# Gate chunks by twos beside the retention: one base block in place of two

## The chip, the cores and the metric

The kernel runs on one core of a Trainium2 chip. The core has TensorE (matrix products, PE in the profile), VectorE (DVE), ScalarE (ACT), GpSimd (POOL) and SyncE (SP), which here issues most transfers. 16 DMA engines move data between the chip's main memory and SBUF. The metric is the time of one execution on the device in microseconds (us).

## The reference

One layer of a hybrid encoder over 256 tokens of width 2048, in float32. In short form below. A normalised input h goes through one wide projection into two token mixers, multi-scale retention (8 heads) and a gated delta rule (16 heads). Each mixer's output is gated by projections of h, and the two are merged by per-channel sigmoid gates. Cross-attention into 256 memory tokens and a squared-ReLU MLP follow.

```python
proj = h @ w_in
(rq, rk, rv, rg, gqkv, ga, gb, gz, gate_a, gate_b) = jnp.split(proj, np.cumsum(IN_SPLITS)[:-1].tolist(), axis=-1)
...
yr = silu(rg) * group_norm(retention(rope(rq), rope(rk), rv))
...
yg = silu(gz) * gated_rms_norm(gated_delta_rule(...))
merged = sigmoid(gate_a) * yr + sigmoid(gate_b) * yg
x = x + merged @ w_out
```

What matters here are the gate projections: h (256 x 2048) times the columns of `w_in` that make rg, gz, gate_a and gate_b, taken in chunks of 512 columns.

## The kernel before

Every float32 operand is split into two parts (`whi`, `wlo` for weights, a "quad" of high and low parts for tokens), and a product is three matmuls: high by high, high by low, low by high. A block of weights is 512 rows by 512 columns (1 MB). It comes by DMA as a tile `raw` of 128 partitions x 2048. ScalarE copies its halves to `whi`, VectorE subtracts for `wlo` (L990 and L991 in the code of this change), and TensorE multiplies 128 tokens by 512 columns at a time.

The mixer runs in four groups (`for j in range(5)`, the last turn only finishes). In each, the delta rule's blocks are projected, then the delta-rule gate of the group before, then `retention(j, yr)`, then `gate_retention(j, yr)`. The delta rule's own core (`gdn_core`) is a generator whose pieces run between the gate's products, a piece at each `step()`.

In groups 1, 2 and 3, and for the last delta-rule gate, the gate's two chunks of 512 columns are computed together by `two_chunks`. Let n be the chunk (0 or 1) and q the block of 512 rows of the weight (0 to 3); `load(n, q)` and `lines(n, q, h)` name such a block. Blocks q = 2 and 3 are multiplied in the plain way (`plain`). For q = 0 and 1 the two chunks and the two halves of the tokens form 2 x 2 blocks, and seven block products do the work of eight. Some take sums of tokens (`summed`, made beforehand by `sums_of_tokens`), some take sums of weight blocks. With b11 = (0, 0), b12 = (1, 0), b22 = (1, 1) and b21 = (0, 1) the weight sums are built in two tiles, each of two halves of 128 x 1024:

- x: first b12 + b11, then b22 is added (x2), then b21 (x4)
- y: b12 + b22

Three ways of building them occur. `load_parts` loads a block on SP's queue. `add_parts` has GpSimd issue a DMA that adds a block from main memory to what stands in the tile. `add_to` has VectorE add a block that is in SBUF anyway. The argument `moved` names the sums that go by adding DMA: in groups 1 to 3 these are x2, x4 and y, and x1 (b12 + b11) is VectorE's. In the last delta-rule gate x1, x2 and x4 go by DMA, and y is VectorE's.

The tiles have no room of their own: x and y take tags of tiles that are idle then. In groups 1 to 3, x has `kq` and `lw`, and y has `qk` and `tw` (`kq`: keys and queries of the delta rule; `lw`, `tw`: operands of its triangular solve; `qk`: queries and keys of the retention). In the last delta-rule gate x has `pairs` and `x_a`. A tile with `bufs=1` is given to its next user when its last reader is done; for `tw` the next user is the clearing on GpSimd (L765) for the following group's solve.

The order of each engine's instructions is worked out when the kernel is built, by a scheduler that simulates the engines. `tc.high_priority` moves loads, splits and additions forward, `tc.issue_after` keeps one instruction behind another. TensorE's order inside `two_chunks` is fixed by the list `ends`.

Lines to follow: L966 (load of a half on SP), L971 (adding DMA on GpSimd), L977 (VectorE's sum), L982 (load of `raw`), L990 and L991 (split), L998 (matmuls), L273 (a power on GpSimd, whose result VectorE needs at L858), L765 (clearing of `tw`).

Of the kernel before, what the change touches and what calls it, by code (L numbers as in the profile page):

```python
# [54 lines left out]
def trunk(ctx: ExitStack, tc: tile.TileContext, x_f, mem_f, positions, lead_f, small_f, w_blocks, w_chunks, w_ga,  # L55
# [3 lines left out]
    act, vec, pool, pe = nc.scalar, nc.vector, nc.gpsimd, nc.tensor  # L59
# [886 lines left out]
        vec.tensor_add(sv[:, 3], a12, sv[:, 1])  # L946
        split([a[:, i, :] for a in s_in], xs[:, 1, :])

    def two_chunks(chunks, evacs, before=None, moved=("x2", "x4", "y"), places=("kq", "lw")):

# [1 line left out]
        shared, p5 = bank("c"), bank("c")  # L954
        kept_back.append(None)
        x, y = ([mx.tile([P, 1024], F32, name=n + e, tag=tag, bufs=1) for e, tag in zip("ab", tags)]
                for n, tags in (("x", places), ("y", ("qk", "tw"))))
        opened, ends = set(), []

        def lines(n, q, h):  # L960
            return w_chunks[chunks[n], q][:, h * 1024:(h + 1) * 1024]

        def load_parts(to, n, q):
            with tc.high_priority(offset=100000), tc.issue_after(fetched[-1]):
                for h in range(2):
                    fetched.append(nc.sync.dma_start(to[h], lines(n, q, h)).ins)  # L966

        def add_parts(to, n, q):
            with tc.high_priority(offset=100000):
                for h in range(2):  # L970
                    pool.dma_start(to[h], lines(n, q, h), accum_op=ALU.add)  # L971

        def add_to(to, src):
            with tc.high_priority(offset=100000):
                for h in range(2):
                    with tc.issue_after(latest["lo"]):
                        vec.tensor_add(to[h], to[h], src[h])  # L977

        def load(n, q):
            raw = wp.tile([P, 4 * 512], F32, name="raw", tag="raw", bufs=3)  # L980
            with tc.high_priority(offset=100000):
                fetched.append(nc.sync.dma_start(raw, w_chunks[chunks[n], q]).ins)  # L982
            return raw[:, 0:1024], raw[:, 1024:2048]
# [25 lines left out]
        def plain(n, q, by_rows=False):  # L1009
            halves = parted(load(n, q))  # L1010
            for c, (i, t) in enumerate([(i, t) for t in range(NT) for i in range(4)] if by_rows else
                                       [(i, t) for i in range(4) for t in range(NT)]):
                ins = triple(own[n][t], [a[:, i, t * P:(t + 1) * P] for a in h1[q]],
                             [a[:, i % 2, :] for a in halves[i // 2]], (n, t))
                if c % 4 == 3:
                    ends.append(ins)
                    step()
# [18 lines left out]
                before(q)  # L1036

        plain(0, 2)
        load_parts(x, 1, 0)
        if "x1" in moved:  # L1040
            add_parts(x, 0, 0)
            load_parts(y, 1, 0)
        b11 = load(0, 0)
        product(shared, part(0, 0), b11, "shared")
        if "x1" not in moved:
            add_to(x, b11)
        with tc.high_priority(offset=50000):
            u = kept_sum("vh", shared)
        u1, u3 = u[:, 0], u[:, 1]
        product(p5, summed(0), x, "p5")  # L1050
        add_parts(x, 1, 1)
        plain(0, 3)
        if "x1" not in moved:
            load_parts(y, 1, 0)
        if "y" in moved:
            add_parts(y, 1, 1)
        b22 = load(1, 1)
# [1 line left out]
        product(shared, summed(1), x, "shared")  # L1059
        add_parts(x, 0, 1)  # L1060
        if "y" not in moved:
            add_to(y, b22)
        with tc.high_priority(offset=50000):
            d = kept_sum("vl", shared)
        others(1)
# [19 lines left out]
    def gates():  # L1085
# [22 lines left out]
        def of_retention(j, yr):  # L1108
            if j in (1, 2, 3):
                two_chunks((H_RG + j, H_TA + j), (silu_gate(yr), sig_gate(yr)))  # L1110
                return
            chunk(h1, cols(w_chunks, H_RG + j), silu_gate(yr))
            chunk(h1, cols(w_chunks, H_TA + j), sig_gate(yr))

        def of_delta_rule(j, yr, yg, quad, before=None):
            if j in (3,):
                spare.append(lambda: tuple(mx.tile([P, 1024], F32R, name=nm, tag=tag, bufs=1)
                                           for nm, tag in (("whx", "r4"), ("wlx", "g_a"))))
                two_chunks((H_GZ + j, H_TB + j), (silu_gate(yg), sig_gate(yg, yr)), before, ("x1", "x2", "x4"),
                           ("pairs", "x_a"))  # L1120
                spare.clear()
            else:
                chunk(h1, cols(w_chunks, H_GZ + j), silu_gate(yg))
                chunk(h1, cols(w_chunks, H_TB + j), sig_gate(yg, yr), before=before, cuts=2 if before else 1)
            to_feature(lambda t, f: yg[:, t, f * P:(f + 1) * P], quad)
# [190 lines left out]
    b11, b12, b22, b21 = (a[:, c:c + 8, :].rearrange("p k s -> p (k s)") for a in (rt, tr) for c in (0, 8))  # L1316
# [342 lines left out]
```

## Time and profile before

| what | value |
|---|---|
| median of 3 runs | 2033.4 us (2032.68 to 2033.46) |
| the profiled execution's own time | 2031.94 us |
| its span, first to last instruction | 2030.1 us |
| granted TensorE clock, mean | 0.999 |
| bytes moved by DMA | 422.03 MB, 208 GB/s on average |
| adding DMAs on GpSimd (L971) | 24 of 512 KB each |
| loads of halves on SP (L966) | 16 of 512 KB each, 4 each for xa, xb, ya, yb |
| VectorE's sums (L977) | 8, about 1.22 us each |

A row of the timeline gives the start in us from the beginning of the span, the length in us, engine, line, operation, output <- inputs (the ends a and b of x and y are their two halves), and in brackets the idle time before it with what ended it. "SPq" is the issue of a transfer on SP's queue. "DMA to landing" is the time from a transfer's issue to its arrival.

### The profile page before, as it was taken

Reading aid. Unit: us, or ns where it says so; the run is one execution under the profiler, and the core shown is the slowest. Engines: PE = TensorE matmul, PEld = TensorE weight load, DVE = VectorE, ACT = ScalarE, POOL = GpSimd, SP = SyncE. Lnnn points to the kernel's source line nnn. Section 1 sums busy time; section 2 is a strip of 40 time slices with the busy share of each in tenths; the row PEclk is TensorE's granted clock in tenths of the full one; section 3 lists DMA queues with packets and bytes.
Section 4 is the critical chain, followed back from the end, with each engine's and each line's share of the span. In section 5 each row is a group of like instructions: output and inputs, shape, how many; then the busy total and the mean of one; then the engine's idle time right before and its main releaser. Section 6 shows DMA issues by size and latency. Waiting matters only on the chain.

```text
span 2030.1 us, 28640 instructions
## 1 busy us (share of the span) xinstructions
PE 2019.0 (99%) x10742; PEld 1740.0 (86%) x10742; DVE 1617.3 (80%) x2507; ACT 1239.0 (61%) x2029; POOL 65.3 (3%) x73
## 2 busy tenths in 40 slices
PE   9999999999999999999999999999999999999998
PEld 7888888988888888888888899888888888888886
DVE  5887788879778887788887665777887887888788
ACT  6655765675567556755665565566557656656665
POOL 0000000000100010000200000000000000000000
PEclk9999999999999999999999999999999999999999
DMA  8578556455945585556976554567546546555661
GB/s 332 214 269 283 187 184 200 158 190 188 283 168 182 192 264 188 184 185 232 275 227 227 209 189 160 180 219 264 207 145 239 214 149 227 194 201 174 236 232 62
DMA packets 84683, 422.03 MB, mean 208 GB/s; under 512 B 17072, under 2 KB 25152, under 8 KB 40256
## 3 DMA queue, kind: packets, MB, share of 16 engines
q1 hardware_dynamic: 80656, 406.93, 57.3%
q0 software_dynamic: 3456, 12.58, 3.4%
q8 instruction: 84, 1.38, 0.3%
q10 hardware_dynamic: 432, 0.69, 0.1%
q14 instruction: 55, 0.45, 0.1%
HBM read 406.52 MB, written 11.55 MB: 206 GB/s over the span
## 4 chain that ended last, share of the span: by engine, by line
PE 96%; DVE 2%; DMA 1%; issue 1%; ACT 0%; SPq 0%; POOLq 0%; DVEq 0%; POOL 0%; ACTq 0%
PE s L217 51%; PE s L1404 8%; PE b L1404 7%; PE s L998 6%; PE s L174 5%; PE s L175 5%; PE s L173 5%; PE b L998 2%; PE s L406 1%; PE s L408 1%; PE s L407 1%; PE b L802 1%; PE b L145 1%; PE b L835 1%; PE b L144 1%; PE b L146 1%
## 5 line engine op out<-in xcount | busy, mean ns | idle before, releaser
L217 PE MATMUL s<-q,whi 128*128 128x512 f32 x2824 | 971.3, 391 | 0.0
L128 ACT ACTIVATE whi<-raw 128x1024 fp32r<-128x1024 f32 x535 | 567.3, 1061 | 419.6 <-PE s L217 219.1
L129 DVE TENSOR_TENSOR wlo<-raw,whi 128x1024 fp32r<-128x1024 f32 x535 | 652.0, 1221 | 214.2 <-ACT whi L128 210.5
L217 PE MATMUL s<-q,wlo 128*128 128x256 f32 x2824 | 765.0, 281 | 0.1
L217 PEld LDWEIGHTS s<-q,whi 128*128 128x128 f32 x2824 | 521.5, 188 | 100.6
L217 PEld LDWEIGHTS s<-q,wlo 128*128 128x128 f32 x2824 | 528.6, 188 | 13.6 <-DVE wlo L129 0.5
L174 PE MATMUL s<-wlo,q 128*128 128x512 f32 x448 | 176.3, 394 | 0.0
L175 PE MATMUL s<-whi,q 128*128 128x512 f32 x448 | 174.7, 390 | 0.0
L173 PE MATMUL s<-whi,q 128*128 128x512 f32 x448 | 158.9, 390 | 0.0
L226 ACT ACTIVATE bo<-s 128x256 f32<-128x256 f32 x192 | 73.1, 381 | 110.0 <-PE s L217 110.0
L1404 PE MATMUL s<-whi,q 128*128 128x512 f32 x384 | 122.1, 389 | 0.0
L227 DVE TENSOR_TENSOR bo<-bo,s 128x256 f32<-128x256 f32 x192 | 79.7, 415 | 41.0 <-ACT bo L226 40.6
L173 PEld LDWEIGHTS s<-whi,q 128*128 128x128 f32 x448 | 84.0, 188 | 17.5
L175 PEld LDWEIGHTS s<-whi,q 128*128 128x128 f32 x448 | 84.2, 188 | 16.7
L174 PEld LDWEIGHTS s<-wlo,q 128*128 128x128 f32 x448 | 84.2, 188 | 16.6
L1427 DVE TENSOR_TENSOR wlo<-rt,whi 128x1024 fp32r<-128x1024 f32 x55 | 67.4, 1225 | 35.8 <-ACT whi L1426 35.4
L998 PE MATMUL s<-whi,q 128*128 128x512 f32 x296 | 94.3, 390 | 0.0
L217 PE MATMUL s<-q,whx 128*128 128x512 f32 x248 | 86.6, 390 | 0.0
L1404 PEld LDWEIGHTS s<-whi,q 128*128 128x128 f32 x384 | 72.1, 188 | 15.0
L1426 ACT ACTIVATE whi<-rt 128x1024 fp32r<-128x1024 f32 x55 | 58.2, 1059 | 41.8 <-PE s L1404 29.4
L1404 PE MATMUL s<-wlo,q 128*128 128x512 f32 x192 | 74.7, 389 | 0.0
L991 DVE TENSOR_TENSOR wlo<-raw,whi 128x1024 fp32r<-128x1024 f32 x52 | 63.3, 1222 | 10.3 <-ACT whi L990 9.9
(427 smaller groups left out, 2970.7 us busy)
## 6 DMA issues: line engine op xcount, KB each, us to landing
raw<-w_ff SPq DMA_DIRECT2D x96, 1024.0 KB
raw<-w_chunks SPq DMA_DIRECT2D x76, 1024.0 KB
raw<-w_blocks SPq DMA_DIRECT2D x64, 1024.0 KB
raw<-w_xk SPq DMA_DIRECT2D x16, 1024.0 KB
raw<-w_out SPq DMA_DIRECT2D x16, 1024.0 KB
raw<-w_xq SPq DMA_DIRECT2D x16, 1024.0 KB
raw<-w_xo SPq DMA_DIRECT2D x16, 1024.0 KB
rt<-w_ff SPq DMA_DIRECT2D x16, 1024.0 KB
```

The lines of the kernel that those rows point to most:

```text
L128: latest["hi"] = act.activation(hi[:, cs], src[:, cs], AF.Copy).ins
L129: latest["lo"] = vec.tensor_sub(lo[:, cs], src[:, cs], hi[:, cs].bitcast(F32)).ins
L173: pe.matmul(o, xh, wh, start=first, stop=False)
L174: pe.matmul(o, xh, wl, start=False, stop=False)
L175: pe.matmul(o, xl, wh, start=False, stop=last)
L217: ins = pe.matmul(ps[b][:, :S] if part else ps[b], halves[h][part][:, i, b * P:(b + 1) * P], x[:, kk % 4, :], start=kk == 0 and not part, ...
L226: act.activation(o, ps[b][:, S:], AF.Copy)
L227: vec.tensor_add(o, o, ps[b][:, :S])
L991: latest["lo"] = vec.tensor_sub(lo, src, hi.bitcast(F32)).ins
L998: ins = pe.matmul(o, lhs[l], rhs[r], start=key not in opened, stop=False, skip_group_check=True).ins
L1404: ins = pe.matmul(o, lhs[l], rhs[r], start=key not in opened, stop=last and j == 2, skip_group_check=True).ins
L1427: latest["lo"] = vec.tensor_sub(lo, raw[:, c:c + 1024], hi.bitcast(F32)).ins
```

## The change

`two_chunks` gets the tags of both tiles as arguments. Where VectorE makes the first sum of x, the base block b12 is loaded once, into y, and VectorE writes x = y + b11 into x's tile, where before b12 was loaded into x, b11 was added in place, and b12 was loaded a second time, into y. GpSimd's addition of b22 to y then works on the tile that VectorE has read. In groups 1 to 3, y now has the tags `kq` and `lw`, and x has `qk` and `tw`. In the last delta-rule gate x1 still goes by DMA, so both loads stay; x keeps `pairs` and `x_a`, and y gets `kq` and `lw`. `add_to` becomes `add_of`, with any two sources.

```diff
-    def two_chunks(chunks, evacs, before=None, moved=("x2", "x4", "y"), places=("kq", "lw")):
+    def two_chunks(chunks, evacs, before=None, moved=("x2", "x4", "y"), places=("qk", "tw"), bases=("kq", "lw")):
...
-                for n, tags in (("x", places), ("y", ("qk", "tw"))))
+                for n, tags in (("x", places), ("y", bases)))
...
-        def add_to(to, src):
+        def add_of(to, *srcs):
             with tc.high_priority(offset=100000):
                 for h in range(2):
                     with tc.issue_after(latest["lo"]):
-                        vec.tensor_add(to[h], to[h], src[h])
+                        vec.tensor_add(to[h], *(src[h] for src in srcs))
...
         plain(0, 2)
-        load_parts(x, 1, 0)
         if "x1" in moved:
+            load_parts(x, 1, 0)
             add_parts(x, 0, 0)
-            load_parts(y, 1, 0)
+        load_parts(y, 1, 0)
         b11 = load(0, 0)
         product(shared, part(0, 0), b11, "shared")
         if "x1" not in moved:
-            add_to(x, b11)
+            add_of(x, y, b11)
...
         add_parts(x, 1, 1)
         plain(0, 3)
-        if "x1" not in moved:
-            load_parts(y, 1, 0)
         if "y" in moved:
             add_parts(y, 1, 1)
         b22 = load(1, 1)
...
         if "y" not in moved:
-            add_to(y, b22)
+            add_of(y, y, b22)
```

## The prediction

> **What bounds the kernel now.** I read the page first, then the chain of waits by engine, then busy time by windows over the places that the change touches. The page:
>
> ```profile
> span 2030.1 us, 28640 instructions
> ...
> PE 2019.0 (99%) x10742; PEld 1740.0 (86%) x10742; DVE 1617.3 (80%) x2507; ACT 1239.0 (61%) x2029; POOL 65.3 (3%) x73
> ...
> PE 96%; DVE 2%; DMA 1%; issue 1%; ACT 0%; SPq 0%; POOLq 0%; DVEq 0%; POOL 0%; ACTq 0%
> ```
>
> TensorE is busy for 99% of the span, and 96% of the chain that ended last is its own work. The edited code runs in four places: beside retention 1, 2 and 3 (calls 1, 2 and 3: from about 507, 721 and 937 us), and once in the last delta-rule gate. The view by windows, for call 2 and for calls 1 to 3 together, and then for stretches of call 1 with different transfers (columns: time, busy time of TensorE, its weight loads, VectorE, ScalarE, GpSimd, then granted clock, DMA share, GB/s):
>
> ```profile
> 721.00:791.00 70.00, 70.00 (x360) 59.55 (x359) 55.49 (x93) 43.95 (x74) 10.56 (x12) 1.00 0.77 235
> ```
>
> ```profile
> sum 197.00, PE 197.00 PEld 167.68 DVE 159.89 ACT 124.46 POOL 35.02; mean PE 65.67 PEld 55.89 DVE 53.30 ACT 41.49 POOL 11.67
> ```
>
> ```profile
> 530.00:534.50 4.50, 4.50 (x25) 3.83 (x24) 4.42 (x13) 2.02 (x3) 0.72 (x1) 1.00 1.05 187
> 536.00:538.50 2.50, 2.50 (x14) 2.04 (x14) 2.47 (x5) 1.80 (x3) 1.53 (x3) 1.00 1.08 380
> ```
>
> The three windows (507 to 576, 721 to 791, 953 to 1011) are 197.00 us long and TensorE is busy for 197.00 of them. The DMA engines are well filled too (a share of 0.77 in call 2), but nothing on TensorE waits for them. The last two rows price a transfer. From 530 to 534.5 only an adding transfer of GpSimd runs, at 187 GB/s; from 536 to 538.5 a plain load, at 380 GB/s. So one block (1.049 MB) costs 1.049/0.380 = 2.8 us of all engines when loaded and 1.049/0.187 = 5.6 us when added.
>
> A busy TensorE could hide slow matmuls, so I look at their spacing. Two pieces of the chain of waits, in order of time (start, length, instructions), the first where the DMA engines are full, the second where they are half idle, and the window of the second:
>
> ```profile
> 539.12 5.68 PE s L998 x25
> ```
>
> ```profile
> 569.92 6.60 PE s L998 x29
> ```
>
> ```profile
> 570.00:576.00 6.00, 6.00 (x28) 4.98 (x27) 5.33 (x10) 3.71 (x11) 1.01 (x1) 1.00 0.52 173
> ```
>
> 5.68/25 = 0.227 us and 6.60/29 = 0.228 us: traffic doesn't stretch them, so less traffic will not shorten them. (The Trainium skill, TensorE: Matmul & The Clock Gate, "Wait — 56ns, not 53.3ns?", gives 0.2157 us for a warm matmul of 512 columns; by that there would be 0.011 us in each matmul, whose cause the rows above show not to be the transfers.)
>
> **The change, part by part.** *Removed:* in calls 1 to 3 the second load of the base block (two halves, 512 KB each, into y). That is 2.8 us of the DMA engines in each call, 3.1 of 422 MB in all. TensorE waits for no transfer there, so this gives 0 us. What the load's absence moves: the plain loads behind it on SP's queue (the block of b22 first) can land earlier, and TensorE has no use for that.
>
> *Moved in place:* the two sums that VectorE writes. They were in place (x = x + b11), now x = y + b11 into other tiles.
>
> ```profile
> L977 DVE TENSOR_TENSOR xb<-xb,raw x3: 1217/1219/1221, 530.3 to 959.4; 128x1024 f32<-128x1024 f32 x3
> ```
>
> ```profile
> 762.50 1.23 DVE L991 TENSOR_TENSOR wlo<-xb,whi 128x1024 fp32r<-128x1024 f32 x1 [0.61 <-ACT whi L990]
> ```
>
> 1.219 us in place; the same engine's subtraction of this size into a third tile takes 1.23 us. Six instructions by 0.01 us, off TensorE's path: 0 us. The new tiles are those named qk and tw. In call 2 their last readers are long done when the second sum starts at 744.86 us (rows of the timeline, of SP, TensorE and VectorE):
>
> ```profile
> 716.80 0.34 SPq L775 DMA_DIRECT2D scr_t<-tw  x1
> ```
>
> ```profile
> 730.61 0.38 PE L903 MATMUL b<-qk 128*128 128x128 f32 x2
> ```
>
> ```profile
> 744.86 1.22 DVE L977 TENSOR_TENSOR xb<-xb,raw 128x1024 f32<-128x1024 f32 x1
> ```
>
> So VectorE gains no wait. In the last gate only y changes its tile, from the one that y of call 3 had to the one that it now has: the same release, 0 us.
>
> *Added wait 1.* GpSimd may add b22 into y only after VectorE has read y for x. Before, y was a tile of its own, and its addition ran ahead of the sum. GpSimd's rows in call 2, the start of the same addition in all calls, and the landing of x's addition:
>
> ```profile
> 742.13 0.85 POOL L971 DMA_DIRECT2D yb<-w_chunks  x1 [0.38 <-issue]
> ...
> 751.78 0.86 POOL L971 DMA_DIRECT2D xb<-w_chunks  x1 [0.96 <-DVE ve L924]
> ```
>
> ```profile
> L971 POOL DMA_DIRECT2D yb<-w_chunks x3: 852/857/877, 526.3 to 957.6; - x3
> ```
>
> ```profile
> L971 POOL DMA_DIRECT2D xb<-w_chunks x1: 860/860/860, 751.8 to 751.8; - x1
> ...
> DMA to landing us min/median/max: 8.8/8.8/8.8
> ```
>
> The second half of y's addition moves from 742.13 to 744.86 + 1.22 = 746.08 us, 3.95 us later; in call 1 from 526.3 to 531.5 (5.2), in call 3 from 957.6 to 960.6 (3.0). Behind it on GpSimd stands x's addition of b22 at 751.78; 4.9 us are left for an instruction of 0.86, so its issue doesn't move. But its transfer is behind y's on the DMA engines. It lands at 751.78 + 8.8 = 760.6 now. Who takes it, in call 2 (ScalarE's part of the split; VectorE's part is the row of 762.50 above; then the first matmul that needs it):
>
> ```profile
> 761.40 1.06 ACT L990 ACTIVATE whi<-xb 128x1024 fp32r<-128x1024 f32 x1 [0.86 <-PE s L998]
> ```
>
> ```profile
> 765.13 0.40 PE L998 MATMUL b<-wlo,sh 128*128 128x512 f32 x1
> ```
>
> ScalarE starts at 761.40, released by TensorE and not by the transfer: 0.8 us of slack. The split ends at 763.73, the matmul needs it at 765.13: another 1.4. TensorE therefore stalls only if x lands more than 2.2 us later than now. For calls 1 and 3:
>
> ```profile
> L971 POOL DMA_DIRECT2D xb<-w_chunks x1: 855/855/855, 537.3 to 537.3; - x1
> ...
> DMA to landing us min/median/max: 7.8/7.8/7.8
> ```
>
> ```profile
> 546.90 1.06 ACT L990 ACTIVATE whi<-xb 128x1024 fp32r<-128x1024 f32 x1 [0.86 <-PE s L998]
> ```
>
> ```profile
> L971 POOL DMA_DIRECT2D xb<-w_chunks x1: 867/867/867, 966.4 to 966.4; - x1
> ...
> DMA to landing us min/median/max: 8.6/8.6/8.6
> ```
>
> ```profile
> 975.91 1.06 ACT L990 ACTIVATE whi<-xb 128x1024 fp32r<-128x1024 f32 x1 [0.86 <-PE s L998]
> ```
>
> Landings 545.1 and 975.0, slack 1.8 and 0.9; with the same 1.4 behind it (the stages repeat to 0.01 us) TensorE stalls from 3.2 and 2.3 us.
>
> How much later will x land? No row shows it. *Lower end:* below nothing, -2.8 us in each call, if the removed load's engine time comes off the queue ahead of x; that is no gain for TensorE. *Upper end:* y's whole shift passes on, 5.2, 4.0 and 3.0 us, so stalls of 2.0, 1.8 and 0.7, together 4.5 us. Between them, if the shift passes on and the removed 2.8 us comes off it, x is 2.4, 1.2 and 0.2 us late. I take some 2 us in each call, nearest to the largest of these: the row of y's shift is the nearer one, since its addition now starts by its issue and not by the queue. 2 us is under all three limits: stall 0.
>
> *Added wait 2.* x now holds the tile tw until its last split. GpSimd clears tw for the next group as soon as y (its holder before) is split. Rows of GpSimd and VectorE in call 2:
>
> ```profile
> 777.21 0.94 POOL L765 MEMSET tw<- 32x1024 f32 x1 [12.33 <-DVE wlo L991]
> 778.28 1.03 POOL L273 TENSOR_TENSOR ro<-qe,nhalf_pow 128x4 f32<-128x4 f32 x1
> ```
>
> ```profile
> 780.51 1.12 DVE L858 SCALAR_TENSOR_TENSOR yg<-b,ro,small 128x128 f32<-128x128 f32 x4
> 781.55 1.22 DVE L991 TENSOR_TENSOR wlo<-xb,whi 128x1024 fp32r<-128x1024 f32 x1
> ```
>
> The clearing moves from 777.21 to 781.55 + 1.22 = 782.77 us. Queued behind it is ro, which yg waits for on VectorE, and yg stands ahead of that very split. In this order the two queues would wait for each other, so the scheduler has to put ro ahead of the clearing, which costs nothing, or yg behind the split (rival B). tw is next used by the following group's solve, tens of us later.
>
> *Sum:* 0 (load) + 0 (sums) + 0 (wait 1) + 0 (wait 2) = 0 us. The profiled execution took 2031.94 us (its span 2030.1 and 1.84 around it), 1.46 less than the median of the three runs, 2033.4 (2032.68 to 2033.46). The sum holds for either; I forecast the median, 2033.4 us.
>
> **The rivals.** *A, slower: x arrives late.* One mechanism, at the product of the third token sum with x, deciding from a landing 2.2 us later (call 2; 3.2 and 2.3 in the others). With the full shift passed on it costs 4.5 us. If x also has to share the engines with the next plain load, it costs one load's time more in each call:
>
> ```profile
> 738.46 17.47 SPq L982 DMA_DIRECT2D raw<-w_chunks  x3
> ```
>
> The third of these loads is issued at about 738.46 + 17.47 - 0.33 = 755.6, while x's addition is under way. Then x is 5.2, 4.0 and 3.0 plus 2.8 us late; less the limits 3.2, 2.2 and 2.3 this is 4.8 + 4.6 + 3.5 = 12.9 us: 2037.9 to 2046.3 us. Against it: in call 1 an addition alone (187 GB/s) and a load alone (380) follow each other in the windows above, so queues are served by turns of whole transfers and not mixed. For it: the slack is only 0.8 us at ScalarE. (The Trainium skill, DMA: Bandwidth & Descriptors, "Queues, rings and completion order", has each engine go round robin between its queues by packets; by that x and the load would share, the dearer end. The rates of the windows speak against it here.) Chance 0.12, of which 0.09 costs over 0.2%.
>
> *B, the clearing's queue.* The scheduler might keep ro behind the clearing and move yg behind the split instead. Then ro ends at 782.77 + 0.94 + 1.03 = 784.7 and yg at 785.9, and the PSUM bank that yg reads is free that late. The matmuls that follow in such a bank:
>
> ```profile
> L851 PE MATMUL b<-y,alt x8: 275/275/275, 782.7 to 784.2; 128*128 128x128 f32 x8
> ```
>
> They would start 785.9 - 782.7 = 3.2 us late, in calls 1 and 2 (call 3 clears nothing): 6.4 us, 2039.8 us. Chance 0.03.
>
> *C, faster.* Loads that land earlier would have to end a wait of TensorE; with 197.00 us busy of 197.00 there is none to end, and outside the calls DVE 2% and DMA 1% of the chain are 61 us that no edited line touches. Only another order of instructions could bring over 4 us: about 2028. Chance 0.03.
>
> **How the numbers follow.** A measurement of this kernel can tell 0.2%, 4.1 us, from no change. The forecast has 0.82 (within about 1 us of 2033.4), A 0.12, B 0.03, C 0.03. Over 0.2% slower: 0.09 of A and 0.03 of B, 0.12. Within: 0.82 and 0.03 of A, 0.85. Faster: 0.03. The range goes from 2032.3 (1.1 us below, the spread of the runs and a little) to 2037.9, the full shift of y in all three calls; outside lie the dearer part of A, B and C, under 2 in 10.
>
> **What would show it.** The changed profile should have four issues of ya and yb by SP, as before, but only one load of x, that of the last gate, and 418.9 MB in place of 422.0. TensorE should be busy for the whole of the three windows. y's addition should start right after the sums, and x's should land 0 to 3 us later than now, with ScalarE's split of xb released by TensorE. If that split waits for DMA and TensorE shows a gap before the product with x, it was A. If VectorE's yg stands behind the split of xb, it was B. A time under 2029 or a different order of TensorE's instructions would prove the forecast wrong altogether.

## The result and the profile after

The changed kernel takes 2043.51 us in the median (2042.54 to 2044.0, 6 runs); the kernel before, beside it, 2033.09 us (2032.22 to 2033.52, 6 runs). The ratio is 1.0052 (95% interval 1.0041 to 1.0063): **slower by 10.4 us**, and outside the range that was given. The profiled execution took 2042.54 us. Its page (span, busy time by engine, the chain that ended last by engine, and the bytes moved):

```profile
span 2040.7 us, 28632 instructions
...
PE 2023.9 (99%) x10742; PEld 1743.4 (85%) x10742; DVE 1617.0 (79%) x2507; ACT 1237.8 (61%) x2029; POOL 63.7 (3%) x73
...
DMA packets 83819, 418.89 MB, mean 205 GB/s; under 512 B 16976, under 2 KB 25056, under 8 KB 39392
...
PE 94%; DVE 3%; DMA 2%; issue 1%; ACT 0%; POOLq 0%; DVEq 0%; POOL 0%; ACTq 0%
```

The 3.1 MB are gone, as forecast. But TensorE is still "99% busy" in a span that is 10.6 us longer: that line would hide the loss. The chain shows it: TensorE 94% in place of 96%, DMA 2% and VectorE 3% in place of 1% and 2%.

**Where the time went.** VectorE's second sum (L977, second half) marks the same point of each call. Its start in calls 1 and 3 (first and last of three), then in call 2, in the changed kernel:

```profile
L977 DVE TENSOR_TENSOR xb<-yb,raw x3: 1217/1217/1219, 531.5 to 966.1; 128x1024 f32<-128x1024 f32 x3
```

```profile
L977 DVE TENSOR_TENSOR xb<-yb,raw x1: 1217/1217/1217, 748.8 to 748.8; 128x1024 f32<-128x1024 f32 x1
```

Before, these points stood at 530.3, 744.9 and 959.4 us. The delay is 1.2 us ahead of call 1, then 3.9 and 6.7, and 10.6 at the end of the span. So calls 1, 2 and 3 cost about 2.7, 2.8 and 3.9 us. The 1.2 us come from the first 20 us of the kernel, where nothing was edited. In the runs below the same sum stands between 530.1 and 533.8 us.

What stops TensorE in the calls is one place, the one of rival A. The view of TensorE's waits of the changed kernel (what it waited for, us in total, times, longest):

```profile
PE b L998 <- ACT whi L990: 3.2, 3, 1.1
PE b L998 <- DVE wlo L991: 2.5, 4, 0.8
```

Before, neither row existed. In call 1 these are the six matmuls with the second half of x, behind eight small matmuls of L802; in the timeline of the kernel before and then of the changed kernel:

```profile
549.50 1.00 PE L802 MATMUL b<-u,pairs 128*128 128x64 f32 x8
...
551.79 0.62 PE L998 MATMUL s<-whi,q 128*128 128x512 f32 x2
```

```profile
551.06 1.00 PE L802 MATMUL b<-u,pairs 128*128 128x64 f32 x8
553.14 0.50 PE L998 MATMUL b<-whi,sh 128*128 128x512 f32 x1 [1.08 <-ACT whi L990]
554.40 0.50 PE L998 MATMUL b<-wlo,sh 128*128 128x512 f32 x1 [0.76 <-DVE wlo L991]
...
555.68 0.62 PE L998 MATMUL s<-whi,q 128*128 128x512 f32 x2
```

From the small matmuls to the next block: 2.29 us before, 4.62 now. The waits in brackets explain 1.84 of these 2.33 us; the rest shows as length of the matmuls beside them (0.50 us and a wider spacing), which is a part of why TensorE's busy time rose too (2019.0 to 2023.9). ScalarE, whose split TensorE waits for, was released by TensorE before; now it is the transfer:

```profile
552.03 1.06 ACT L990 ACTIVATE whi<-xb 128x1024 fp32r<-128x1024 f32 x1 [3.29 <-DMA xb<-w_chunks]
```

How late that transfer is, in calls 1, 2 and 3 of the changed kernel (issue of x's addition of b22, then issue to landing):

```profile
L971 POOL DMA_DIRECT2D xb<-w_chunks x1: 852/852/852, 538.8 to 538.8; - x1
...
DMA to landing us min/median/max: 13.2/13.2/13.2
```

```profile
L971 POOL DMA_DIRECT2D xb<-w_chunks x1: 857/857/857, 755.9 to 755.9; - x1
...
DMA to landing us min/median/max: 13.4/13.4/13.4
```

```profile
L971 POOL DMA_DIRECT2D xb<-w_chunks x1: 869/869/869, 973.5 to 973.5; - x1
...
DMA to landing us min/median/max: 12.6/12.6/12.6
```

| | call 1 | call 2 | call 3 |
|---|---|---|---|
| sum's start to x's landing, before (us) | 14.8 | 15.7 | 15.6 |
| the same, after | 20.5 | 20.5 | 20.0 |
| x is later by | 5.7 | 4.8 | 4.4 |
| limit that the prediction worked out | 3.2 | 2.2 | 2.3 |
| stall that follows | 2.5 | 2.6 | 2.1 |
| stall measured | 2.7 | 2.8 | 3.9, of which 1.7 by the clock (last section) |

The limits hold to 0.3 us, once the clock's part is taken off call 3. The lateness was the error: the prediction took 2 us.

### The profile page after: what moved, and what is told of

Same layout as the page of the kernel before. It is cut to its first block, busy times and chain, and to the rows that moved or that the text cites. A ratio compares the mean times of both kernels' runs of the same rounds, so it can differ in the third digit from the quotient of the medians.

```text
span 2040.7 us, 28632 instructions
## 1 busy us (share of the span) xinstructions
PE 2023.9 (99%) x10742; PEld 1743.4 (85%) x10742; DVE 1617.0 (79%) x2507; ACT 1237.8 (61%) x2029; POOL 63.7 (3%) x73
## 3 DMA queue, kind: packets, MB, share of 16 engines
q0 software_dynamic: 3456, 12.58, 3.4%
## 4 chain that ended last, share of the span: by engine, by line
PE 94%; DVE 3%; DMA 2%; issue 1%; ACT 0%; POOLq 0%; DVEq 0%; POOL 0%; ACTq 0%
PE s L217 52%; PE s L1402 7%; PE b L1402 7%; PE s L174 5%; PE s L173 5%; PE s L175 5%; PE s L998 4%; DMA xb<-w_chunks 2%; PE b L998 1%; PE s L406 1%; PE s L407 1%; PE s L408 1%; PE b L705 1%; DVE wlo L991 1%; PE b L835 1%
## 5 line engine op out<-in xcount | busy, mean ns | idle before, releaser
L217 PEld LDWEIGHTS s<-q,wlo 128*128 128x128 f32 x2824 | 528.8, 188 | 13.5 <-DVE wlo L129 0.4
```

Of the source, the lines that this page charges most:

```text
L217: ins = pe.matmul(ps[b][:, :S] if part else ps[b], halves[h][part][:, i, b * P:(b + 1) * P], x[:, kk % 4, :], start=kk == 0 and not part, ...
```

## The experiments

Each expectation names its theories by letters of its own. The kernel before stood beside the first four at 2032.79 us (25 runs) and beside the last two at 2032.85 us (15 runs).

**1. x's addition ahead of y's.** The changed kernel, with y's addition queued behind x's on GpSimd, and nothing else:

```diff
-                    pool.dma_start(to[h], lines(n, q, h), accum_op=ALU.add)
+                    latest["added"] = pool.dma_start(to[h], lines(n, q, h), accum_op=ALU.add).ins
...
-            add_parts(y, 1, 1)
+            with tc.issue_after(latest["added"]):
+                add_parts(y, 1, 1)
```

> The changed kernel, with GpSimd's addition into y queued behind its first addition into x (one order on GpSimd alone). Theory Q (x's addition lands late because it is queued on the DMA engines behind y's, which now starts after VectorE's sum): x lands about as early as in the kernel before, 6.7 to 8.8 us after its issue, TensorE has no gap before the product with x, and the time falls by 9 to 10 us to 2033 to 2034 us; y lands near 550 us in call 1, needed at about 558. Rival P (the new places of x and y, or the sum that is no longer in place, slow something): the order on GpSimd changes nothing, 2042 to 2044 us. Rival S (the missing load shifts the loads on SP's queue): the same, 2042 to 2044 us.

Measured: 2033.46 us (10 runs), ratio to the kernel before 1.0004 (0.9994 to 1.0013). Call 1 of this kernel, the sum, then x's addition and its landing:

```profile
L971 POOL DMA_DIRECT2D xb<-w_chunks x1: 877/877/877, 538.2 to 538.2; - x1
L977 DVE TENSOR_TENSOR xb<-yb,raw x1: 1220/1220/1220, 531.0 to 531.0; 128x1024 f32<-128x1024 f32 x1
...
DMA to landing us min/median/max: 6.9/6.9/6.9
```

x lands 14.1 us after the sum, 0.7 earlier than in the kernel before, and the two rows of TensorE's waits are gone. The whole loss comes back by the order of two transfers on one queue; the load that was removed, the out-of-place sums and the exchanged tiles all stay in. So x's addition, queued behind y's, is the cause. The order has its price at y, which lands at 554.5 us in call 1 in place of the 550 expected, still ahead of its split (second half at 560.4).

**2. The tiles alone.** The kernel before, with the tiles of x and y exchanged, both loads and the sum in place:

```diff
-places=("kq", "lw")):
+places=("qk", "tw"), bases=("kq", "lw")):
...
-                for n, tags in (("x", places), ("y", ("qk", "tw"))))
+                for n, tags in (("x", places), ("y", bases)))
```

> The kernel before, with the tiles of x and y exchanged (x in qk and tw, y in kq and lw; both loads, the sum in place). Theory Q: y's addition doesn't wait for the sum, so 2032.5 to 2034 us. Rival P by the places: 2042 to 2044 us, or a part of the 10.4 us. Rival S: 2033 us.

Measured: 2034.48 us (10 runs), ratio 1.0008 (0.9999 to 1.0017). At most 3.5 us, by the upper end of the interval, and no difference that could be told from none. In its trace (2036.01 us, the slowest of the ten runs) x lands 14.0, 14.3 and 15.6 us after the sum in calls 1 to 3, no later than in the kernel before, and TensorE waits for 0.7 us in all. The places are not what cost 10 us.

**3. The removed load kept, as a load that nobody uses.** The changed kernel, with b12 still loaded into x's tile and then overwritten by the sum:

```diff
         plain(0, 2)
+        load_parts(x, 1, 0)
         if "x1" in moved:
-            load_parts(x, 1, 0)
             add_parts(x, 0, 0)
```

> The changed kernel, with the removed load kept as a load into x whose data VectorE's sum overwrites: the traffic of before, the waits of the changed kernel. Theory Q: the traffic was not what made it slow, so no better than the changed kernel, 2043 to 2045 us. Rival S: 2033 to 2035 us.

Measured: 2048.96 us (4 runs, 2044.56 to 2049.03), ratio 1.0074 (1.0059 to 1.0089): some 5 us slower than the changed kernel, and above the 2045 of the expectation. The trace is of the fastest of the four runs. TensorE's waits in its three calls (500 to 1070 us):

```profile
PE b L998 <- ACT whi L990: 4.4, 4, 1.5
PE b L998 <- DVE wlo L991: 3.7, 5, 0.8
```

With the load back the kernel is not faster, so the missing traffic was not what disturbed it. Nor does the load make x later: x lands 20.6, 20.3 and 20.1 us after the sum, as in the changed kernel (20.5, 20.5, 20.0). The 2.4 us by which these waits exceed those of the changed kernel (5.7) all stand in call 1. What brings them about, and what costs the three slower runs another 4.4 us, is not shown.

**4. No adding transfer for y.** The changed kernel, with VectorE adding b22 into y:

```diff
-moved=("x2", "x4", "y"), places=("qk", "tw"), bases=("kq", "lw")):
+moved=("x2", "x4"), places=("qk", "tw"), bases=("kq", "lw")):
```

> The changed kernel, with b22 added to y by VectorE from the block that is in SBUF anyway, in calls 1 to 3, in place of GpSimd's adding transfer: 3.1 MB less by adding DMA, six sums of 1.22 us more on VectorE. Theory Q: x's addition has no other in front of it and lands 2 to 4 us earlier than in the kernel before; no gap of TensorE before x's product; 2033 to 2034 us, unless VectorE's 2.4 us in each call make a later split late (up to 2.4 us in each call, 2040 us). Rivals P and S: 2042 us or more.

Measured: 2036.01 us (10 runs), ratio 1.0016 (1.0006 to 1.0026). The wait ahead of x's product is gone, and a smaller one has come (TensorE's waits in the three calls):

```profile
PE s L998 <- DVE wlo L991: 1.3, 2, 0.6
PE s L217 <- DVE gth L1087: 0.7, 2, 0.3
```

x lands 13.5, 13.3 and 13.1 us after the sum, 1.3, 2.4 and 2.5 earlier than in the kernel before. Most of the loss is back without y's transfer, which points at the queue as well. TensorE now waits for VectorE, which has two more sums of 1.22 us in each call; that these make its later splits late fits, but no run separates it.

Experiment 1 shows that the order of the two transfers is the cause, but not why x is 5.7 us late instead of some 2. The changed kernel's transfers in call 1, by windows (columns as in the prediction; the last is GB/s):

```profile
534.00:537.00 3.00, 3.00 (x18) 2.56 (x16) 3.00 (x11) 2.37 (x3) 1.36 (x3) 1.00 0.84 281
...
547.00:550.00 3.00, 2.94 (x13) 2.08 (x12) 1.45 (x2) 1.31 (x2) 0.00 (x0) 1.00 1.04 311
550.00:552.00 2.00, 2.00 (x13) 1.70 (x12) 0.20 (x1) 0.00 (x0) 0.88 (x1) 1.00 1.02 387
```

and the two issues right behind the sum, on GpSimd and on SP:

```profile
533.09 1.23 POOL L971 DMA_DIRECT2D yb<-w_chunks  x1
```

```profile
532.84 0.33 SPq L982 DMA_DIRECT2D raw<-w_chunks  x1
```

An addition alone ran at 187 GB/s and a load alone at 380; 281 and 311 lie between. The view of transfers by queue tells them apart: q0 carries GpSimd's additions (12.58 MB in the whole kernel, the 24 of 512 KB) and q1 SP's loads. Its rows (packets, MB, share of the 16 engines), first call 1 from 534 to 537 us, then from 540 to 545, then from 546 to 550:

```profile
q1 hardware_dynamic: 103, 0.84, 84.4%
```

```profile
q0 software_dynamic: 280, 1.02, 106.4%
```

```profile
q0 software_dynamic: 116, 0.45, 55.9%
q1 hardware_dynamic: 97, 0.79, 49.1%
```

So right behind the sum a load runs alone, then the additions alone, and from 546 on, while x's second half is still to land (552.0), addition and load run mixed. The sum frees two transfers at once: y's addition, and, with the `raw` buffer of b11, the plain load of (1, 2). In call 2 the load goes first as well. In call 3 the two share the engines from the start (970 to 975 us):

```profile
q0 software_dynamic: 112, 0.46, 53.4%
q1 hardware_dynamic: 115, 0.94, 49.5%
```

The last two experiments each hold a load back by a transfer of 64 bytes out of x on SP's queue, which waits for x's addition.

**5. b21's load held until x has landed.**

```diff
+        def landed(t):
+            with tc.high_priority(offset=100000), tc.issue_after(fetched[-1]):
+                fetched.append(nc.sync.dma_start(dram.tile([1, 16], F32, name="seen", tag="seen", bufs=2), t[0:1, 0:16]).ins)
...
-            with tc.high_priority(offset=100000):
+            with tc.high_priority(offset=100000), tc.issue_after(fetched[-1]):
                 fetched.append(nc.sync.dma_start(raw, w_chunks[chunks[n], q]).ins)
...
-        add_parts(x, 0, 1)
+        if "x1" in moved: add_parts(x, 0, 1)
...
         plain(1, 2)
+        if "x1" not in moved: landed(x[1]); add_parts(x, 0, 1)
         b21 = load(0, 1)
```

The line in `load` keeps every later load behind the held one, so the load of (1, 3) waits too; x's addition of b21 (x4) moves behind the small transfer.

> The changed kernel, but in calls 1 to 3 the plain load of b21 isn't issued until x's addition of b22 has landed (a transfer of 64 bytes out of x on SP's queue waits for it, and b21's load is kept behind that). Theory S (x's second half is late because it shares the DMA engines with b21's load, seen as 311 GB/s from 547 to 550 us): without the sharing the second half of x lands some 2 us earlier in each call, its wait of 1.1 us at TensorE and the one for VectorE behind it go to 0 to 0.5 us per call, and the time falls from 2043.5 to 2034-2037 us. Theory O (x is late because y's addition starts late, after the plain load of b12's neighbour (1,2) has gone ahead): x still lands at nearly the same time, 2041-2043.5 us. Both equally: 2038-2040.

Measured: 2034.82 us (10 runs), ratio 1.0011 (1.0002 to 1.0021). Sum and landing in call 1, then the window in which the two had been mixed:

```profile
L971 POOL DMA_DIRECT2D xb<-w_chunks x1: 857/857/857, 538.2 to 538.2; - x1
L977 DVE TENSOR_TENSOR xb<-yb,raw x1: 1218/1218/1218, 531.0 to 531.0; 128x1024 f32<-128x1024 f32 x1
...
DMA to landing us min/median/max: 10.6/10.6/10.6
```

```profile
547.00:550.00 3.00, 3.00 (x15) 2.40 (x14) 1.65 (x2) 1.86 (x4) 0.88 (x1) 1.00 0.30 57
```

x lands 17.8 us after the sum: 3.0 later than before in place of 5.7, just under the limit of 3.2. In calls 2 and 3 it is 2.0 and 1.5 us later, under the limits of 2.2 and 2.3. TensorE's two waits are gone. What is left of the loss, 2 us, is new: behind call 3 VectorE's `yg` now waits for GpSimd's `ro`, a split stands behind it, and TensorE waits for the split (timelines of VectorE and TensorE):

```profile
999.58 1.13 DVE L858 SCALAR_TENSOR_TENSOR yg<-b,ro,small 128x128 f32<-128x128 f32 x4 [2.95 <-POOL ro L273]
```

```profile
1001.90 0.50 PE L998 MATMUL s<-wlo,q 128*128 128x512 f32 x1 [1.44 <-DVE wlo L991]
```

**6. The load of (1, 2) held as well.** The same transfer and the same line in `load`, one load earlier:

```diff
-        add_parts(x, 0, 1)
+        landed(x[1]) if "x1" not in moved else None; add_parts(x, 0, 1)
```

> The changed kernel, but in calls 1 to 3 the plain load of (1,2), and b21's behind it, isn't issued until x's addition of b22 has landed (the same 64-byte transfer, one load earlier), so that no load stands beside either addition. Theory O: y's first packets come some 2.8 us earlier, right after the issue at about 533 us instead of 537.5, x lands 4 to 5 us earlier, and the wait before x's product is gone (0 in all calls). If the delay between the issue and the first packets is GpSimd's own (theory L), they still come at about 537 and x lands only as much earlier as without sharing (some 2 us). Under both the load of (1,2) is now late, landing about 550-552 us, and its split can make TensorE wait up to 2 us per call: 2033-2039 us. The time decides little here; the first packets of y and the landing of x decide.

Measured: 2039.75 us (6 runs), ratio 1.0037 (1.0024 to 1.0049); the upper end of the expectation was 2039. In call 1, with the two windows behind y's issue:

```profile
L971 POOL DMA_DIRECT2D xb<-w_chunks x1: 855/855/855, 538.9 to 538.9; - x1
L977 DVE TENSOR_TENSOR xb<-yb,raw x1: 1220/1220/1220, 531.7 to 531.7; 128x1024 f32<-128x1024 f32 x1
...
DMA to landing us min/median/max: 8.5/8.5/8.5
```

```profile
534.00:537.00 3.00, 3.00 (x18) 2.52 (x16) 3.00 (x11) 2.26 (x3) 1.36 (x3) 1.00 0.91 152
537.00:540.00 3.00, 3.00 (x17) 2.54 (x17) 2.97 (x6) 2.30 (x3) 1.80 (x3) 1.00 1.05 191
```

Without a load beside it y's addition runs from 534 us on, so its late start in the changed kernel was the load's doing and no delay of GpSimd's. x lands 15.7 us after the sum, only 0.9 later than before; in calls 2 and 3 it is 0.3 later and 0.5 earlier. The time is lost to the held load: the waits stand now at a plain block (output `s`, not `b`).

```profile
PE s L998 <- DVE wlo L991: 2.6, 4, 1.0
PE s L998 <- ACT whi L990: 2.2, 2, 1.2
```

The three kernels size the parts of x's lateness, when the loads are taken away in this order (us):

| | call 1 | call 2 | call 3 |
|---|---|---|---|
| changed kernel, both loads beside the additions | 5.7 | 4.8 | 4.4 |
| experiment 5, without b21's (and (1, 3) behind it) | 3.0 | 2.0 | 1.5 |
| experiment 6, without either | 0.9 | 0.3 | -0.5 |

So **sharing with b21's load is 2.7 to 2.9 us in each call, the load of (1, 2) ahead of or beside y's addition 1.7 to 2.1, and y's later addition by itself under 1**. No experiment beat the kernel before; the best, 1, can't be told from it.

## Why the prediction was wrong

By its own steps:

- *Removed load, 0 us:* right. In experiment 1, where it is the main thing left of the change, nothing is won. The 5 us that the load costs in experiment 3 are open.
- *Sums out of place, 0 us:* right; 1.217 us in place of 1.219. VectorE gained no wait on the tiles, and exchanging them alone cost nothing that could be told (experiment 2).
- *Added wait 2, the clearing of `tw`, 0 us:* right. GpSimd has `ro` ahead of the clearing, in call 2:

```profile
785.06 1.03 POOL L273 TENSOR_TENSOR ro<-qe,nhalf_pow 128x4 f32<-128x4 f32 x1 [12.19 <-DVE qe L855]
789.61 0.94 POOL L765 MEMSET tw<- 32x1024 f32 x1 [3.51 <-DVE wlo L991]
```

- *Added wait 1, y's addition starts right after the sums:* right in the issue (533.09 us, behind a sum that starts at 531.5 and lasts 1.22). The limits of 3.2, 2.2 and 2.3 us for x's landing: right to 0.3 us.
- *Added wait 1, "I take some 2 us in each call ... stall 0":* **this step failed.** The measured lateness is 5.7, 4.8 and 4.4 us, over even the upper end of the step (5.2, 4.0, 3.0). The term that the step put at nothing is the sharing of the engines with b21's load, 2.7 to 2.9 us in each call. Without it x is 3.0, 2.0 and 1.5 us late (experiment 5), each under its limit. So 2 us would have been a fair size for the rest, but by luck, since its reasons did not hold. "Its addition now starts by its issue and not by the queue" was wrong: the sum that releases y's addition also releases the load of (1, 2), which ran first or beside it (1.7 to 2.1 us). And the removed load's 2.8 us could not come off x's queue: in call 1 before, the load was issued at 518.6 us, over 11 us ahead of the sum, and in the changed kernel the engines stand idle from 531 to 533 us (share 0.00), just ahead of these transfers.
- *Rival A:* it had the place, the wait, and the sharing with the next plain load, at 2.8 us in each call. Its other term, y's full shift of 5.2, 4.0 and 3.0, was too large: x without b21's load is 3.0, 2.0 and 1.5 us late, most of that by the load of (1, 2), which A did not name. So its dearer price was 12.9 us (2037.9 to 2046.3), and 10.4 us were measured, 1.7 of them by the clock. Its chance of 0.12 was too low because of the argument against it, "queues are served by turns of whole transfers and not mixed". That was read from one stretch of call 1 before. There the load, issued at 531.59 us, did wait until y's addition was nearly through (535.2); but one stretch is no rule, and in the changed kernel both forms stand in one call, a load alone at 281 GB/s and the two mixed at 311.

The rule that spoke for A was quoted with it: the Trainium skill, DMA: Bandwidth & Descriptors, "Queues, rings and completion order", has each engine go round robin between its queues by packets. The mixed stretches agree, and so does experiment 5, in which x lands 2.7 us earlier without the sharing. Other stretches do not show it: b21's load is issued at 542.34 us, and until 545.8 only the additions' queue has packets. In experiment 5 the same load, with nothing beside it, has packets some 0.8 us after its issue. Why two queues sometimes take turns by whole transfers and sometimes mix is open.

Rivals B and C did not happen: the clearing moved as forecast, and TensorE's instructions stand in the same order as before.

## What to carry to other kernels

A wait moved onto an unimportant transfer was paid here by what stands behind it in its queue, and made dearer by the loads that run beside the two: list them all, and issue the urgent transfer first (here that order was worth the whole 10 us). Where an unknown delay is compared with a slack, decide by the upper end of the delay, not by the value one favours; here the upper end exceeded the slack in all three calls, and that alone said that "no change" was not safe. And a TensorE that is 99% busy before and after says nothing of such a loss; the chain of waits and the rows by place do.

## What was not expected of the hardware

**After a few short waits TensorE's clock dropped.** In call 3 of the changed kernel (columns: time, busy time of TensorE, its weight loads, VectorE, ScalarE, GpSimd, granted clock, DMA share, GB/s):

```profile
986.00:989.00 3.00, 1.21 (x6) 0.72 (x6) 1.71 (x2) 2.80 (x3) 0.18 (x1) 1.00 1.02 326
...
990.00:992.00 2.00, 2.00 (x6) 1.54 (x5) 1.72 (x3) 1.54 (x2) 0.00 (x0) 0.50 0.88 119
...
989.40:995.00 5.60, 5.60 (x21) 4.48 (x20) 3.64 (x5) 2.17 (x4) 0.28 (x1) 0.70 0.97 197
```

TensorE idled for 1.8 us of three, and a microsecond later it ran at half its clock. In the 5.6 us of the last row 0.30 of the clock is missing: 1.7 us. That leaves 2.2 of call 3's 3.9 us for its waits, near the 2.1 that follows from x's lateness. Calls 1 and 2 have the same two waits and kept a clock of 1.00. In experiment 3 it fell in call 3 again (0.66 on average):

```profile
989.00:994.00 5.00, 3.63 (x8) 2.66 (x9) 3.83 (x4) 3.31 (x5) 0.86 (x1) 0.66 0.92 197
```

The Trainium skill, TensorE: Matmul & The Clock Gate, "HAM oscillation — how this bites in real kernels", gives idle gaps of over some 3.4 us as what brings the clock down. Here the clock fell after two gaps of 1.0 and 0.8 us with one matmul between them, so by these rows the limit can be lower than that section has it. Why calls 1 and 2 were spared was not tested. The number of such drops in an execution may also be what spreads the times of one kernel: of the 4 runs of experiment 3 the one with a mean clock of 0.998 took 2044.56 us, the three with 0.996 about 2049.
